# Strassen's rule for the output projection of the mixers in a two-layer encoder

## The chip, the cores and the metric

The kernel runs on one core of a Trainium2 chip. The metric is the device time of one execution in microseconds, the median of several runs. The engines of the core are named as in the profile: PE does matmuls (PEld is its weight load), DVE and ACT are the vector and the scalar engine, POOL and SP here mostly issue DMAs.

## The reference

The program is the trunk of an encoder: 16 learned tokens are put before 512 input tokens (528 rows of 1024 features), two layers follow, and a norm at the end.

```python
for l in range(DEPTH):                       # DEPTH = 2, D_MODEL = 1024, D_FF = 2816
    h = h + 0.5 * swiglu(rmsnorm(h, g[l, 0]), w_gate[l, 0], w_up[l, 0], w_down[l, 0])
    h = h + mixer(rmsnorm(h, g[l, 1]), ...)
    h = h + 0.5 * swiglu(rmsnorm(h, g[l, 2]), w_gate[l, 1], w_up[l, 1], w_down[l, 1])
return rmsnorm(h, final_norm)[:, N_META:]

def mixer(z, ...):                           # a, b: 528 x 512 each
    a, b = gla_branch(...), attention_branch(...)
    y = sigmoid(g_a + b_merge[0]) * (a @ w_pa) + sigmoid(g_b + b_merge[1]) * (b @ w_pb)
    return y @ w_out                         # y: 528 x 1024, w_out: 1024 x 1024
```

All is float32. This case is about the last line, `y @ w_out`.

## The kernel before

Activations lie transposed: a chunk of h is 128 features by all tokens (528; in the mixer of the last layer and after it only the 512 that the output needs), and there are 8 chunks. A float32 product is done as three: operand and weights are split into a high part that PE takes as it is and a low part with the rest, and high x high, high x low and low x high are added in PSUM. The helper `split` does it for operands (ACT casts at L476, DVE subtracts at L477), `Weights.make` for a slab of weights of 128 x 1024 (ACT `whi` at L310, DVE `wlo` at L311). Slabs come by DMAs that SP issues (L287, or `block` for the FFN), a few slabs ahead of their use. The order of use is a list made ahead, `weight_plan`, which `W.next` and `W.op` walk.

The FFNs already use Strassen's rule in the Winograd form. The operand of the FFN's first products is made by `Norm.pair` out of two finished chunks of h: seven slices (`xc`, high and low), each a quarter or a sum of quarters. Seven products numbered "1" to "7" replace eight, each with a weight block that is a quarter (11, 12, 22 for "1", "2", "4") or a sum of quarters. These sums are made outside PE: partly on DVE, partly by DMAs from POOL that add into their target (`add`, L224), with negations on ACT (L219). The FFN's last products (`fast_down`, L745) do the same with three groups of merged gate and up values, in two halves of the output columns each (`dq` 0 and 1); a group is 4, 4 or 3 pairs long, and each product adds its PSUM result into h (L753).

The end of the mixer is plain. For m in 0 to 7 the two gates of a chunk are made, `pa` and `pb` are products of four slabs each (L1255, L1256), the gates are multiplied with them on DVE (L1259), added (L1261) and split (L476, L477). Then, for each of the 8 chunks of output, eight slabs of `w_out` are multiplied with the eight chunks of y (L1267; the matmuls are at L488), the result is added into h (L587) and `done(m)` is called: a square of the chunk on ACT (L522) and a sum of squares on DVE (L526), and after every second chunk `pair`, which makes the slices for the next FFN (L532 to L551). The next FFN begins with the matmuls at L621.

Each engine serves its instructions in order; the order is that in which the program is written, changed by a scheduler within priorities.

Of the kernel before, what the change touches and what calls it, by code (L numbers as in the profile page):

```python
# [10 lines left out]
F32 = mybir.dt.float32  # L11
# [30 lines left out]
GROUPS = (4, 4, 3)  # L42
ALL_FAST = [(0, 0), (1, 0)]
# [16 lines left out]
def ffn_steps(f):  # L60
# [3 lines left out]
    for g, n in enumerate(GROUPS):  # L64
# [7 lines left out]
        for i in range(n):  # L72
# [5 lines left out]
            if not more and g < fast:  # L78
# [7 lines left out]
                turns = [("S", g, *t, 3) for t in zip(AB, "16273465734")]  # L86
# [16 lines left out]
def weight_plan():  # L103
# [20 lines left out]
    for l in range(DEPTH):  # L124
# [37 lines left out]
NOP = NPAIR + QUADS * len(GROUPS)  # L162
# [20 lines left out]
def wide(i):  # L183
    return SLAB if i < NPAIR else 2 * P * GROUPS[(i - NPAIR) // QUADS]


class Weights:
# [93 lines left out]
    def fetch(self, upto):  # L281

        while self.fetched < min(upto, len(self.loads)):
            load = self.loads[self.fetched]
            if isinstance(load, int):
                w = self.raw.tile([P, SLAB], F32, tag="raw", name=f"raw{load}")
                self.nc.sync.dma_start(w, self.wts[load])  # L287
                self.raws[self.fetched] = w
            elif load[2] in DIRECT:
# [62 lines left out]
def build(tc, ctx, xt, wts, win, par, w2, const, umask, out):  # L352
# [240 lines left out]

    pending, closing = [load_constants], [None]

    def ffn(l, f, norm, done, following):
# [67 lines left out]
        def hidden(st, p, m):  # L664
# [11 lines left out]
            if p < sum(GROUPS[:fast]):  # L676
                if p // 4 not in raw:
                    raw[p // 4] = [quarter("g") for _ in range(4)]
                for q in range(2):
# [7 lines left out]
        def quarter(tag, dtype=F32):  # L687
            return slots[tag].tile([P, 2 * T], dtype, tag=tag, name=nm(tag))[:, : 4 * w].rearrange(
                "p (k c) -> p k c", k=4)

        def operand(g, c, ks=None):

            ks = ks or slice(0, GROUPS[g])
            src = raw[g][{"1": 0, "2": 2, "5": 0, "6": 0, "7": 1, "3": 3, "4": 2}[c]]
            if (g, c) not in sets:
                tag = "c" if c in "56" else "g"
                sets[g, c] = [quarter(tag, F32R) for _ in range(2)]
            hi, lo = [t[:, ks] for t in sets[g, c]]
            if c == "3":
                S.activation(hi, src[:, ks], AF.Copy, scale=-1.0)  # L700
                V.scalar_tensor_tensor(lo, src[:, ks], -1.0, hi.bitcast(F32), ALU.mult, ALU.subtract)
            else:
                cast = S.copy(hi, src[:, ks])
                if g == len(GROUPS) - 1:
                    prev_act[0] = cast.ins
                V.tensor_tensor(lo, src[:, ks], hi.bitcast(F32), ALU.subtract)  # L706

        def difference(g, into, a, b, ks=None):
            r, ks = raw[g], ks or slice(0, GROUPS[g])
            V.tensor_tensor(r[into][:, ks], r[a][:, ks], r[b][:, ks], ALU.subtract)  # L710

        def operands_of(g, ks, order):
            for c in order:
                if c == "5":
                    difference(g, 0, 1, 0, ks)
                operand(g, c, ks)

        def operands_behind(g, dq, c):
            if (dq, c) == (1, "1"):
                difference(g, 1, 1, 3)  # L720
                operand(g, "7")
            elif (dq, c) == (1, "2"):
                operand(g, "3")
                difference(g, 2, 2, 0)
                operand(g, "4")

        def fast_down(g, dq, c, part):
            last = sum(GROUPS[: g + 1]) - 1
            kinds = ("ss", "s2") if last % 2 == 0 else ("s2", "ss")
            st = made.setdefault(("S", g, dq), {})  # L730
            where = {"2": "Y", "5": "Z", "3": "Z"}.get(c, "X")
            begin = c in "125"
            if part != 2:
                if begin:
                    st[where] = pair(kinds[{"Y": 0, "Z": 1, "X": dq}[where]] == "s2")
                st["w"] = st.get("w", {})
                st["w"][c] = W.op((l, f), NPAIR + QUADS * g + dq, c, ahead=AHEAD_MADE - 1)
            acc = st[where][:, :, :w]
            hi, lo = st["w"][c]
            xs = sets[g, c]  # L740
            n = GROUPS[g]
            for k in {1: range(n - 1), 2: range(n - 1, n), 3: range(n)}[part]:
                for j in range(2):
                    for i, (a, b) in enumerate(((hi, 0), (hi, 1), (lo, 0))):
                        closing[0] = TE.matmul(acc[:, j], a[:, j, k], xs[b][:, k], start=bool(begin and k == 0 and i == 0),  # L745
                                               stop=k == n - 1 and i == 2, skip_group_check=not begin).ins
            if part == 1:
                return
            st["w"].pop(c)
            for m, q in {"1": [(0, 0)], "2": [(0, 0)], "5": [(1, 1)], "6": [(0, 1)], "3": [(0, 1)], "7": [(1, 1)],  # L750
                         "4": [(1, 0)]}[c]:
                to = hall[:, 4 * dq + 2 * m : 4 * dq + 2 * m + 2, q * w : (q + 1) * w]
                V.tensor_tensor(to, to, acc, ALU.add)  # L753
            if g == len(GROUPS) - 1:
                if c in "34":
                    ready.extend([4 * dq + 2 * (c == "4"), 4 * dq + 2 * (c == "4") + 1])
                for _ in range(len(ready) if (dq, c) == CLOSING[-1] else min(len(ready), PACE)):
                    m = ready.pop(0)
                    lower_h(m, rs)
                    done(m)  # L760
            if dq == 1:
                sets.pop((g, c))
            with tc.high_priority() if c == "1" else nullcontext():
                operands_behind(g, dq, c)
# [24 lines left out]
        for i, step in enumerate(steps):  # L789
# [16 lines left out]
            elif step[0] == "O":  # L806
                g, last = step[1:]
                n_k = GROUPS[g]
                ks = slice(n_k - 1, n_k) if last else slice(0, n_k - 1)
                operands_of(g, ks, "152")  # L810
                difference(g, 0, 3, 0, ks)
                if last:
                    for ks in (slice(0, 2), slice(2, n_k)):
                        operand(g, "6", ks)
# [365 lines left out]
    def mixer(l, norm, done, following):  # L1180
# [67 lines left out]
        y = []  # L1248
        for m in range(KC):
            ga, gb = gates[2 * m : 2 * m + 2]  # L1250
# [183 lines left out]
```

## Time and profile before

| | |
|---|---|
| median of 3 runs | 2187.26 us (2186.92 to 2187.61) |
| span of the profiled execution | 2185.6 us |
| PE, DVE, ACT, POOL busy | 2149.1, 1802.6, 1245.9, 119.0 us |
| end of the mixer of layer 0: merge, projection | 676.5 to 718.9, 718.9 to 765.6 us |
| projection of layer 1 | 1791.8 to 1836.2 us |

Times are from the start of the span. "idle before" and the brackets name what ended a wait of the engine. A matmul's printed length is longer than the distance from one matmul to the next, since they are pipelined; distances are the safer number. The granted TensorE clock (PEclk) is 1.00 in the stages spoken of here.

### The profile page before, as it was taken

The numbers are of one execution on the slowest core, as the hardware profiler recorded it, in microseconds if no ns is written. First come the engines' busy times: TensorE is split into PE (matmuls) and PEld (weight loads), VectorE is DVE, ScalarE is ACT, GpSimd is POOL, SyncE is SP. The second block draws the span as 40 slices with busy tenths as digits, with TensorE's granted clock in tenths as the row PEclk, the third lists the DMA queues.
The fourth block names the chain that finished last, engine by engine and source line by source line (L and its number), as shares of the span: only waits on it lengthen the run. The fifth ranks groups of instructions, "written<-read, shape, count | busy, mean of one in ns | idle before, by whom it ended". The sixth has DMA issues, their size and how long they took to land.

```text
span 2185.6 us, 40161 instructions
## 1 busy us (share of the span) xinstructions
PE 2149.1 (98%) x16434; PEld 2056.1 (94%) x16434; DVE 1802.6 (82%) x2751; ACT 1245.9 (57%) x1844; POOL 119.0 (5%) x140
## 2 busy tenths in 40 slices
PE   7999999999999999999999999999999999999998
PEld 7999999989999999999999999988788888999997
DVE  8887979776976689888789979797779767997986
ACT  8545556444784556454575455574557836554544
POOL 1100000000000000010010000000000001000100
PEclk9999999999999999999999999999999999999999
DMA  9866755212113467676567667553121146775751
GB/s 286 218 195 182 202 154 139 82 51 76 49 40 123 130 177 180 202 185 183 167 162 187 199 181 204 153 140 97 49 78 49 49 135 152 199 204 178 196 162 68
DMA packets 91223, 320.32 MB, mean 147 GB/s; under 512 B 10144, under 2 KB 12576, under 8 KB 91040
## 3 DMA queue, kind: packets, MB, share of 16 engines
q1 hardware_dynamic: 70048, 246.58, 33.9%
q0 software_dynamic: 19584, 69.21, 17.6%
q8 instruction: 129, 2.11, 0.4%
q10 hardware_dynamic: 1408, 1.97, 0.3%
q14 instruction: 54, 0.44, 0.1%
HBM read 294.65 MB, written 2.10 MB: 136 GB/s over the span
## 4 chain that ended last, share of the span: by engine, by line
PE 83%; DVE 9%; ACT 4%; DMA 2%; issue 2%; SPq 0%; DVEq 0%; ACTq 0%
PE ss L621 36%; PE mm L488 15%; PE ss L745 14%; PE ss L488 7%; DVE wlo L311 3%; PE sm L488 2%; DMA w<-win 2%; PE sm L1125 1%; PE ss L1100 1%; ACT whi L310 1%; PE ss L494 1%; DVE h L753 1%; PE sm L1141 1%; PE ss L1101 1%; PE sm L1142 1%
## 5 line engine op out<-in xcount | busy, mean ns | idle before, releaser
L621 PE MATMUL ss<-xc,whi 128*128 128x264 f32 (+1 forms) x4928 | 903.1, 285 | 11.3 <-ACT whi L310 7.4
L621 PEld LDWEIGHTS ss<-xc,whi 128*128 128x128 f32 x4928 | 764.5, 189 | 14.9 <-ACT whi L310 8.0
L621 PE MATMUL ss<-xc,wlo 128*128 128x264 f32 (+1 forms) x2464 | 700.6, 285 | 4.0 <-DVE wlo L311 4.0
L311 DVE TENSOR_TENSOR wlo<-w,whi 128x1024 fp32r<-128x1024 f32 (+2 forms) x355 | 423.7, 1200 | 66.7 <-ACT whi L310 66.3
L621 PEld LDWEIGHTS ss<-xc,wlo 128*128 128x128 f32 x2464 | 465.0, 189 | 5.9 <-DVE wlo L311 5.9
L310 ACT CAST whi<-w 128x1024 fp32r<-128x1024 f32 (+2 forms) x355 | 362.1, 1036 | 169.3 <-PE ss L621 80.1
L488 PE MATMUL mm<-x,whi 128*128 128x264 f32 (+1 forms) x1712 | 385.5, 315 | 0.0
L488 PEld LDWEIGHTS mm<-x,whi 128*128 128x128 f32 x1712 | 278.1, 188 | 16.3 <-issue 1.0
L745 PE MATMUL ss<-g,whi 128*128 128x264 f32 (+1 forms) x1520 | 284.3, 285 | 3.6 <-DVE h L753 1.7
L488 PE MATMUL mm<-x,wlo 128*128 128x264 f32 (+1 forms) x856 | 266.3, 316 | 0.0
L745 PEld LDWEIGHTS ss<-g,whi 128*128 128x128 f32 x1520 | 236.2, 188 | 7.5 <-DVE g L706 3.6
L745 PE MATMUL ss<-g,wlo 128*128 128x264 f32 (+1 forms) x760 | 215.2, 283 | 0.0
L625 ACT COPY c<-ss 128x528 f32<-128x528 f32 (+1 forms) x132 | 78.4, 594 | 239.0 <-PE ss L621 238.7
L310 ACT CAST whi<-raw 128x1024 fp32r<-128x1024 f32 x114 | 119.3, 1048 | 130.7 <-PE mm L488 94.2
L311 DVE TENSOR_TENSOR wlo<-raw,whi 128x1024 fp32r<-128x1024 f32 x114 | 139.0, 1220 | 57.2 <-ACT whi L310 53.2
L488 PEld LDWEIGHTS mm<-x,wlo 128*128 128x128 f32 x856 | 159.6, 188 | 8.5 <-issue 0.5
L745 PEld LDWEIGHTS ss<-g,wlo 128*128 128x128 f32 x760 | 143.0, 188 | 0.0
L224 POOL DMA_DIRECT2D w<-win x64 | 56.1, 876 | 1453.2 <-DVE t L1261 342.0
L745 PE MATMUL ss<-c,whi 128*128 128x264 f32 (+1 forms) x608 | 115.5, 285 | 0.3
L311 DVE TENSOR_TENSOR wlo<-s,whi 128x1024 fp32r<-128x1024 f32 (+1 forms) x94 | 112.2, 1195 | 1.6 <-ACT whi L310 1.4
L467 ACT ACTIVATE c<-c 128x528 f32<-128x528 f32 (+1 forms) x88 | 56.5, 642 | 98.5 <-DVE c L671 98.4
L488 PE MATMUL ss<-g,whi 128*128 128x264 f32 (+2 forms) x516 | 103.6, 310 | 0.0
(270 smaller groups left out, 3379.1 us busy)
## 6 DMA issues: line engine op xcount, KB each, us to landing
w<-win SPq DMA_DIRECT2D x333, 512.0 KB, 4.4
raw<-wts SPq DMA_DIRECT2D x114, 512.0 KB, 3.3
w<-win POOLq DMA_DIRECT2D x60, 512.0 KB, 7.5
s<-win POOLq DMA_DIRECT2D x26, 512.0 KB, 7.5
w<-s POOLq DMA_DIRECT2D x26, 512.0 KB, 6.1
w<-win SPq DMA_DIRECT2D x20, 384.0 KB, 3.6
s<-w POOLq DMA_DIRECT2D x8, 512.0 KB, 7.4
h<-xt SPq DMA_DIRECT2D x3, 528.0 KB, 6.0
```

The source lines that it names most:

```text
L224: self.nc.gpsimd.dma_start(t, src, accum_op=ALU.add)
L310: nc.scalar.copy(hi[:, cs], w[:, cs])
L311: nc.vector.tensor_tensor(lo[:, cs], w[:, cs], hi[:, cs].bitcast(F32), ALU.subtract)
L467: prev_act[0] = S.activation(*args, **kw).ins
L488: TE.matmul(acc.half[i][:width], lhs, rhs[:, acc.spans[i]], start=first, stop=last)
L494: TE.matmul(a, weights, x[:, hs], start=True, stop=True)
L621: TE.matmul(acc[:, j], a[:, j, k], b[:, at], start=bool(begin and k == 0 and i == 0), stop=k == len(x) - 1 and i == 2, skip_group_check=no ...
L625: W.behind = S.copy(part(st, q), acc).ins
L745: closing[0] = TE.matmul(acc[:, j], a[:, j, k], xs[b][:, k], start=bool(begin and k == 0 and i == 0), stop=k == n - 1 and i == 2, skip_gro ...
L753: V.tensor_tensor(to, to, acc, ALU.add)
L1100: TE.matmul(s[:n, i, :HF], lhs, kh[:, hs], start=True, stop=False)
L1101: TE.matmul(s[:n, i, :HF], lhs, kl[:, hs], start=False, stop=True)
```

## The change

The output projection becomes one more group of the scheme that `fast_down` uses. The code of that scheme moves, unchanged in what it does, from the FFN into a class `Sets`, which the FFN and the mixer share. In the mixer

- the merged values of a chunk are not split any more, but written as two token halves into raw quarters (`raw[0]` to `raw[3]`, L1284): chunks with even m into quarters 0 and 1, with odd m into 2 and 3;
- `Sets.operand` and `Sets.difference` make the operands of the seven products out of them: "1", "5", "2" in `begin` (three of the four places of a quarter before m = 6, the last place after the merge loop, and then "6"), "7", "3", "4" behind products of the second column half;
- the projection is 7 products times two column halves, 24 matmuls each, in the order of `MERGED` after (0,"1"), (0,"5") and (0,"2"); 18 matmuls of (0,"1") stand ahead of the last pair of `pa` and `pb`. A product's result goes into two chunks of h at once for half of the tokens (L673, 14 adds of 128 x 2 x 264). `done` follows after products "3" and "4", one chunk per product;
- `w_out` is laid out as quarters. For each column half SP loads five blocks, and four DMAs from POOL add one block into another. One sum is made when the block of "6" has been split: ACT negates the block 12 (L281), and POOL adds block of "6" into it; the result is the weight of "3". The block buffers are opened ahead of the merge loop.

```diff
-        y = []
+        close_pools(pools)
+        opened()
+        own = open_pools("left", c=4)
+        raw = [quarter("c") for _ in range(4)]
+        out = Sets((l, 1), OUT, raw, ("ss", "s2"), {"4": "c"})
+        w = n_out // 2
         for m in range(KC):
+            if m == KC - 2:
+                out.begin(False)
+            if m == KC - 1:
+                out.product(0, "1", 1)
...
-            t = slot("t")
-            V.tensor_tensor(t, ga, gb, ALU.add)
-            y.append(split(t, "g"))
-        close_pools(pools)
+            for q in range(2):
+                cs = slice(q * w, (q + 1) * w)
+                V.tensor_tensor(raw[2 * (m % 2) + q][:, m // 2], ga[:, cs], gb[:, cs], ALU.add)
+        close_pools(banks)
         close_pools(norm.pools)
+        own.update(open_pools("left", psum=("s2",), s2=2))
         following()
-        for m in range(KC):
-            add_to_h(m, product("w_out", Acc(KINDS[m % 4]), y, KC))
-            done(m)
-        close_pools(banks)
+        for c in "52":
+            out.product(0, c, 1)
+        out.begin(True)
+        for c in "152":
+            out.product(0, c, 2)
+        ready = []
+        for dq, c in MERGED:
+            out.product(dq, c, 3)
+            if ready:
+                done(ready.pop(0))
+            if c in "34":
+                ready += [4 * dq + 2 * (c == "4"), 4 * dq + 2 * (c == "4") + 1]
+        for m in ready:
+            done(m)
+        close_pools(own)
```

and, in the class that the FFN shares (its bodies are those that stood in the FFN before):

```diff
+    class Sets:
+        def operand(self, c, ks=None):
...
+                cast = S.copy(hi, src[:, ks])
...
+                V.tensor_tensor(lo, src[:, ks], hi.bitcast(F32), ALU.subtract)
+        def difference(self, into, a, b, ks=None):
+            r, ks = self.raw, ks or slice(0, self.n)
+            V.tensor_tensor(r[into][:, ks], r[a][:, ks], r[b][:, ks], ALU.subtract)
+        def behind(self, dq, c):
+            if (dq, c) == (1, "1"):
+                self.difference(1, 1, 3)
+                self.operand("7")
+            elif (dq, c) == (1, "2"):
+                self.operand("3")
+                self.difference(2, 2, 0)
+                self.operand("4")
+        def product(self, dq, c, part):
...
+                to = hall[:, 4 * dq + 2 * m : 4 * dq + 2 * m + 2, q * w : (q + 1) * w]
+                V.tensor_tensor(to, to, acc, ALU.add)
```

and where the order of the products and the weights is set:

```diff
+MERGED = tuple(zip((1, 0, 1, 0, 0, 0, 1, 1, 1, 1, 1), "16273465734"))
...
+            if m == KC - 1:
+                plan.append(("op", (l, 1), NPAIR + QUADS * OUT, "1"))
             mat("w_pa", (l,), m * P, 0, 4)
             mat("w_pb", (l,), m * P, 0, 4)
-        for m in range(KC):
-            mat("w_out", (l,), m * P, 0, KC)
+        for dq, c in ((0, "5"), (0, "2")) + MERGED:
+            plan.append(("op", (l, 1), NPAIR + QUADS * OUT + dq, c))
```

How this moves instructions, in layer 0. The names: `h` is the residual stream, `xc` the slices of a pair for the next FFN, `wlo` and `whi` the parts of a weight block, `w_01_18`, `s_01_18` a block or a sum of blocks of the second column half of `w_out` (17 is the first), `w_01_0`, `s_01_0` those of the next FFN's first pair of columns, `c` and `g` in the last columns quarters and operands, `t` scratch.

DVE, the end of the projection. Before, the rows between the slices of the third pair (xc_9137) and those of the fourth (xc_9280):

```order
L540 TENSOR_TENSOR xc_9137<-t_9145,xc_9136 128x528
L587 TENSOR_TENSOR h<-h,ss_9154 128x528
L526 TENSOR_TENSOR t_8780<-t_8780,t_9211 128x528
L311 TENSOR_TENSOR wlo_9217<-w_01_1_8870,whi_9216 128x1024
L587 TENSOR_TENSOR h<-h,sm_9214 128x264
L587 TENSOR_TENSOR h<-h,sm_9215 128x264
L526 TENSOR_TENSOR t_8780<-t_8780,t_9272 128x528
L547 TENSOR_TENSOR t_9287<-t_9275 128x264
L548 TENSOR_TENSOR t_9287<-t_9276,t_9287 128x264
L540 TENSOR_TENSOR xc_9280<-t_9275,xc_9279 128x264
L540 TENSOR_TENSOR xc_9280<-t_9276,xc_9279 128x264
```

In the change, between the third (here xc_9270) and the fourth (here xc_9298):

```order
L551 SCALAR_TENSOR_TENSOR xc_9270<-t_9266,xc_9269 128x264
L554 TENSOR_TENSOR t_9277<-t_9266,t_9277 128x264
L556 TENSOR_TENSOR t_9278<-t_9265,t_9266 128x264
L557 TENSOR_TENSOR t_9278<-t_9266,t_9277 128x264
L532 TENSOR_TENSOR t_9051<-t_9051,t_9287 128x528
L546 TENSOR_TENSOR xc_9270<-t_9277,xc_9269 128x528
L546 TENSOR_TENSOR xc_9270<-t_9278,xc_9269 128x528
L532 TENSOR_TENSOR t_9051<-t_9051,t_9290 128x528
L553 TENSOR_TENSOR t_9305<-t_9293 128x264
L317 TENSOR_TENSOR wlo_9325<-w_01_1_9015,whi_9324 128x1024
L546 TENSOR_TENSOR xc_9298<-t_9293,xc_9297 128x264
L546 TENSOR_TENSOR xc_9298<-t_9294,xc_9297 128x264
```

Before, the last products of the projection and the chunks they finish take turns; now four sums of squares and two pairs of slices stand one behind another after the last add into h (L673, six rows further up in that listing).

ACT, where the sums of the weights are negated. Before, in the middle of the projection:

```order
L522 ACTIVATE t_8930<-h 128x528
L310 CAST whi_8935<-raw_8596 128x1024
L219 ACTIVATE s_01_0_8722<-w_01_0_8720 128x1024
L522 ACTIVATE t_8991<-h 128x528
L532 ACTIVATE t_8994<-h,par 128x528
L532 ACTIVATE t_8995<-h,par 128x528
L539 CAST xc_8998<-t_8994 128x264
L539 CAST xc_8998<-t_8995 128x264
L544 ACTIVATE xc_8998<-t_8995 128x264
```

In the change:

```order
L528 ACTIVATE t_9051<-h 128x528
L528 ACTIVATE t_9084<-h 128x528
L223 ACTIVATE s_01_0_8943<-w_01_0_8941 128x1024
L281 ACTIVATE s_01_18_8981<-w_01_18_8541 128x1024
L538 ACTIVATE t_9087<-h,par 128x528
L538 ACTIVATE t_9088<-h,par 128x528
L545 CAST xc_9091<-t_9087 128x264
L545 CAST xc_9091<-t_9088 128x264
L550 ACTIVATE xc_9091<-t_9088 128x264
L545 CAST xc_9091<-t_9099 128x528
L528 ACTIVATE t_9139<-h 128x528
L316 CAST whi_9110<-s_01_18_8981 128x1024
```

`s_01_18_8981` is the weight of (1,"3"): it is negated behind the squares of the first two chunks of h (t_9051, t_9084), and cast (whi_9110) behind the first pair's slices.

PE, where the FFN first needs the fourth pair. In the change:

```order
L706 MATMUL ss_9355<-xc_9269,wlo_9226 128x264
L706 MATMUL ss_9355<-xc_9269,whi_9225 128x264
L706 MATMUL ss_9355<-xc_9270,whi_9225 128x264
L706 MATMUL ss_9355<-xc_9269,wlo_9226 128x264
L706 MATMUL ss_9388<-xc_9091,whi_9324 128x264
L706 MATMUL ss_9388<-xc_9092,whi_9324 128x264
L706 MATMUL ss_9323<-xc_9297,whi_9196 128x264
L706 MATMUL ss_9355<-xc_9297,whi_9225 128x264
L706 MATMUL ss_9388<-xc_9091,wlo_9325 128x264
```

Row by row, 38 matmuls of the FFN stand ahead of the first with xc_9297, the fourth pair; before, 27 stand ahead of it. Over the whole program PE has 16279 matmuls for 16183, DVE 2797 instructions for 2743, ACT 1814 for 1788, POOL 152 DMAs for 136, SP 486 for 482.

More of the change, by code (lines that the diff above doesn't have):

```diff
@@ L42 @@
 GROUPS = (4, 4, 3)
+OUT = len(GROUPS)
+SETS = GROUPS + (KC // 2,)
 ALL_FAST = [(0, 0), (1, 0)]
@@ L85, in ffn_steps @@
                     continue
-                turns = [("S", g, *t, 3) for t in zip(AB, "16273465734")]
+                turns = [("S", g, *t, 3) for t in MERGED]
                 steps += turns[:6]
@@ L161 @@
 NPAIR = FF // P // 2
-NOP = NPAIR + QUADS * len(GROUPS)
+NOP = NPAIR + QUADS * len(SETS)
 PLAN = weight_plan()
@@ L183, in wide @@
 def wide(i):
-    return SLAB if i < NPAIR else 2 * P * GROUPS[(i - NPAIR) // QUADS]
+    return SLAB if i < NPAIR else 2 * P * SETS[(i - NPAIR) // QUADS]
 class Weights:
@@ L288, in fetch @@
                 self.raws[self.fetched] = w
+            elif self.short is None:
+                return
             elif load[2] in DIRECT:
@@ L678, in hidden @@
                     raw[p // 4] = [quarter("g") for _ in range(4)]
+                    last = LAST[p // 4] % 2 == 0
+                    sets[p // 4] = Sets((l, f), p // 4, raw[p // 4], ("ss", "s2") if last else ("s2", "ss"), {"5": "c", "6": "c"})
                 for q in range(2):
@@ L685, in hidden @@
             hid[2 * p + m] = split(u, "g")
[L687 to L725, printed above, removed]
@@ L727, in fast_down @@
-        def fast_down(g, dq, c, part):
[L728 to L747, printed above, removed]
-                return
[L749 to L759, printed above, removed]
-                    done(m)
[L761 to L764, printed above, removed]
@@ L766, in down @@
+        def fast_down(g, dq, c, part):
+            sets[g].product(dq, c, part)
+            if part == 1 or g < len(GROUPS) - 1:
+                return
+            if c in "34":
+                ready.extend([4 * dq + 2 * (c == "4"), 4 * dq + 2 * (c == "4") + 1])
+            for _ in range(len(ready) if (dq, c) == CLOSING[-1] else min(len(ready), PACE)):
+                m = ready.pop(0)
+                lower_h(m, rs)
+                done(m)
         def down(g, m, first, last):
@@ L807, in ffn @@
                 g, last = step[1:]
[L808 to L814, printed above, removed]
+                sets[g].begin(last)
             else:
@@ L1178, in block_pools, with mixer @@
         return pools
-    def mixer(l, norm, done, following):
+    def mixer(l, norm, done, opened, following):
         x, n_out = norm.x, T if l < DEPTH - 1 else SEQ
@@ L1259, in mixer @@
                     V.tensor_tensor(cut(gate), cut(gate), pv, ALU.mult)
[L1260 to L1263 removed]
+            for q in range(2):
+                cs = slice(q * w, (q + 1) * w)
+                V.tensor_tensor(raw[2 * (m % 2) + q][:, m // 2], ga[:, cs], gb[:, cs], ALU.add)
+        close_pools(banks)
         close_pools(norm.pools)
+        own.update(open_pools("left", psum=("s2",), s2=2))
         following()
[L1266 to L1267 removed]
+        for c in "52":
+            out.product(0, c, 1)
+        out.begin(True)
+        for c in "152":
+            out.product(0, c, 2)
[4 more added lines that the diff above has]
+                done(ready.pop(0))
+            if c in "34":
+                ready += [4 * dq + 2 * (c == "4"), 4 * dq + 2 * (c == "4") + 1]
+        for m in ready:
             done(m)
[L1269 removed]
+        close_pools(own)
     fin = Norm(G_FIN)
@@ L1352, in build @@
         close_pools(bp.pop())
-        mixer(l, b, c.chunk_of_pair, lambda: (operand_pools(c, "xc"), bp.append(block_pools())))
+        W.long = W.short = None
+        mixer(l, b, c.chunk_of_pair, lambda: bp.append(block_pools()), lambda: operand_pools(c, "xc"))
         if l < DEPTH - 1:
@@ L1404 @@
         row += 2 * P * n
+    wo = a["w_out"].reshape(DEPTH, KC // 2, 2, P, QUADS, 2, 2, P).transpose(0, 4, 5, 2, 3, 6, 1, 7).reshape(DEPTH, 1, -1, P, SLAB)
+    blocks.append(np.pad(wo, [(0, 0), (1, 0)] + [(0, 0)] * 3))
     win = np.ascontiguousarray(np.concatenate(blocks, axis=2)).reshape(-1, P, SLAB)
```

52 lines of the change are left out of this document (51 added, 1 removed).

## The prediction

> **What bounds the kernel now.** I read the page's first part, then a table of busy time by stage, since the change touches two places of some 45 us, then PE's waits there.
>
> ```profile
> PE 2149.1 (98%) x16434; PEld 2056.1 (94%) x16434; DVE 1802.6 (82%) x2751; ACT 1245.9 (57%) x1844; POOL 119.0 (5%) x140
> ```
>
> PE is busy for 98% of the span, so matmuls that go are worth their full time, as long as nothing makes PE wait. DVE at 82% isn't far behind. The stages, with columns as in the first line:
>
> ```profile
> core 0: us, PE busy (x) PEld busy (x) DVE busy (x) ACT busy (x) POOL busy (x), PEclk, DMA share, GB/s
> 676.50:718.90 42.40, 42.40 (x347) 42.40 (x347) 29.13 (x45) 14.00 (x18) 0.89 (x1) 1.00 0.44 137
> 718.90:765.60 46.70, 46.70 (x388) 46.70 (x386) 31.73 (x56) 26.19 (x40) 4.36 (x5) 1.00 0.55 141
> 1791.80:1836.20 44.40, 44.40 (x193) 35.87 (x191) 30.51 (x52) 25.75 (x40) 4.37 (x5) 1.00 0.55 140
> 330.00:380.00 50.00, 48.68 (x390) 47.69 (x389) 49.36 (x74) 34.08 (x50) 3.22 (x4) 1.00 0.50 132
> ```
>
> The first is the merge of layer 0, the next two are the output projections of layers 0 and 1: PE never stops in them, and DVE idles for a third of the time. The last is the end of the first FFN, whose last products go by Strassen's rule already: there DVE is full and PE loses 1.3 us. At the end of the two projections PE waits once each:
>
> ```profile
> PE ss L621 <- DVE wlo L311: 0.5, 1, 0.5
> ...
> PE ss L621 <- DVE wlo L311: 0.8, 1, 0.8
> ```
>
> **What the matmuls that go are worth.** Layer 0: 384 matmuls, 264 wide, in 46.70 us make 0.1216 us each. Strassen does seven products of 3 x 4 x 2 matmuls for each of two column halves, 336, also 264 wide. 48 x 0.1216 = **5.8 us**. Layer 1: 192 matmuls, 512 wide, in 44.40 us (0.231 each) become 336 that are 256 wide. For that width I take the second layer's next FFN:
>
> ```profile
> 1859.99 0.40 PE L621 MATMUL ss<-xc,whi 128*128 128x256 f32 x2
> ...
> 1861.05 0.40 PE L621 MATMUL ss<-xc,whi 128*128 128x256 f32 x2
> ```
>
> Between these lie nine matmuls (three groups of whi, whi, wlo) in 1.06 us, 0.118 each; 336 x 0.118 = 39.6, so 44.4 - 39.6 = **4.8 us**. Together 10.6 us.
>
> [...] The trace has 231 and 118 ns, a ratio of 0.51, and I go by it.
>
> **What DVE gets.** Halving the number of PE's products costs DVE: operands must be added, split into high and low part, and seven results per half added into h (14 adds of 528 instead of 8 of 528 or pairs of 264); there are 14 weight blocks instead of 8, each with a low half on DVE. And these come after the last gate product: three of the four merged quarters are complete only then. To see whether DVE keeps up, I count its instructions in the new order, in layer 0, from the last gate product to the first slice of the fourth pair of the next FFN's operand (xc_9298), which PE needs after all 318 products that remain of the projection (18 of the 336 stand ahead of the last gate product) and 38 of the FFN. They are 78: 14 low halves of 1024, 29 of 528 (14 adds to h, 7 sums of squares, 8 of the operands), 30 of 264, 5 of 1056. What each takes on a full queue shows where they stand back to back:
>
> ```profile
> 793.99 1.22 DVE L271 TENSOR_TENSOR w<-w,w 128x1024 f32<-128x1024 f32 x1
> 795.13 0.42 DVE L681 TENSOR_TENSOR g<-c,ss 128x264 f32<-128x264 f32 x1
> 795.47 0.42 DVE L681 TENSOR_TENSOR g<-c 128x264 f32<-128x264 f32 x1
> 795.81 0.70 DVE L654 TENSOR_TENSOR c<-c,ss 128x528 f32<-128x528 f32 x1
> 796.43 1.22 DVE L320 TENSOR_TENSOR w<-w,w 128x1024 f32<-128x1024 f32 x1
> ...
> L706 DVE TENSOR_TENSOR g<-g,g 128x1056 fp32r<-128x1056 f32 x12 | 15.0, 1247 | 0.0
> ```
>
> From start to start: 1.14 for 1024, 0.34 for 264, 0.62 for 528; each is some 0.085 shorter than its printed length, so 1056 takes 1.247 - 0.085 = 1.16. 14 x 1.14 + 29 x 0.62 + 30 x 0.34 + 5 x 1.16 = 16.0 + 18.0 + 10.2 + 5.8 = **49.9 us**. In layer 1 each row is 1 to 3% shorter (512 for 528); I take 49.0. PE's work up to there is (318 + 38) x 0.1216 = **43.3 us**, in layer 1 356 x 0.118 = **42.0**. DVE's queue is served in order, so PE must wait for it: at least 6.6 and 7.0 us. In the kernel before, the same stretch has 62 DVE instructions (8 of 1024, 19 of 528, 35 of 264), 32.8 us at these lengths, against 46.7 us of projection and 27 FFN matmuls; that is why it showed only 0.5 and 0.8.
>
> If the lengths as printed held instead (1.22, 0.70, 0.42, 1.25), the queue would be 56.2 us, 6.3 more in each layer; the rows above show the overlap, so I take the lower end.
>
> **What else delays that queue.** Three hand-overs where DVE has just caught up with PE or ACT (the start, the operand of "7", one product's end) at about 0.3 each, an estimate between gaps such as these two; 0.9 in all, between 0 and 3 x 0.77:
>
> ```profile
> 792.85 1.23 DVE L311 TENSOR_TENSOR wlo<-w,whi 128x1024 fp32r<-128x1024 f32 x1 [0.18 <-ACT whi L310]
> ...
> 767.87 0.71 DVE L526 TENSOR_TENSOR t<-t,t 128x528 f32<-128x528 f32 x1 [0.77 <-ACT t L522]
> ```
>
> Then the last weight sum. The block of (1,"3") of the second half is a chain: ACT negates a block (s_01_18_8981), POOL adds another into it by DMA, ACT casts it, DVE takes the low half, as 44th of the 78. In ACT's order this negation stands behind two squares of finished chunks of h (L528 of the change), and these wait for the adds that DVE makes at 22.0 us into its queue.
>
> ```profile
> L522 ACT ACTIVATE t<-h 128x528 f32<-128x528 f32 x40 | 24.1, 636 | 12.3 <-DVE h L587 12.2
> L219 ACT ACTIVATE s<-w 128x1024 f32<-128x1024 f32 x34 | 35.7, 1056 | 6.9 <-DMA w<-win 3.6 <-DVE wlo L311 3.0
> L310 ACT CAST whi<-w 128x1024 fp32r<-128x1024 f32 x333 | 344.7, 1051 | 157.2 <-PE ss L621 75.9 <-PE ss L745 47.5 <-DVE wlo L311 9.3
> ...
> 1436.95 0.84 ACT L277 ACTIVATE s<-w 128x768 f32<-128x768 f32 x1 [0.40 <-DVE wlo L311]
> ...
> 1438.20 0.88 POOL L224 DMA_DIRECT2D s<-w  x1 [5.79 <-ACT s L277]
> ...
> s<-w POOLq DMA_DIRECT2D x8, 512.0 KB, 7.4
> ...
> DMA to landing us min/median/max: 3.8/7.5/11.7
> ```
>
> 22.0 plus 0.6 of hand-over, two squares (1.3), the FFN's negation ahead of it and its own (2.1): 26.0; POOL issues 0.41 after a negation ends (1437.79 to 1438.20): 26.4; landing 7.4 later: 33.8; cast: 34.9. DVE has reached the low half at 30.4 + 0.9 = 31.3. It stands there for **3.5 us**, and behind it all of pairs 1 to 3 of the next FFN. For the landing the ends are 3.8 and 11.7: 0 to 7.8 us lost.
>
> [...]
>
> Behind the fourth pair DVE and ACT are still late: walking the rows on at these durations, PE waits once more for each of two weight blocks' low halves, 1.5 and 0.9 us; I take **2.4**, between 0 and 2.4.
>
> **What I cost at nothing.** In the merge, a split and a 528-wide add per m become two adds of 264: less for DVE, and PE is the bound there (42.40 of 42.40 busy). Four more loads on SP and 16 more DMAs on POOL: the DMA share is 0.44 to 0.55 in these stages, and the loads of the first blocks lie ahead of the merge, as the block buffers are opened there now. If that cover is gone, a late block costs a landing, 7.4 us at most. ACT gets 26 instructions more in all, at 57% busy.
>
> **The sum** (layer 0, layer 1): queue 49.9, 49.0; hand-overs 0.9 each; late sum 3.5 each: 54.3, 53.4. Less PE's work 43.3, 42.0: PE stands for 11.0, 11.4. Tail 2.4 each. Less the waits of before, 0.5 and 0.8, less the matmuls, 5.8 and 4.8: +7.1, +8.2. Together +15.3 us on a span of 2185.6, that is 2200.9; the median of the runs lies 1.7 over that span: **2203 us**.
>
> **The rivals.**
> 1. DVE is the bound, but the sum lands in time (landing at 3.8, or ACT comes to the negation sooner). For it: 3.8 is in the row; against it the median. 15.3 - 2 x 3.5 = +8.3: **2196**.
> 2. DVE keeps pace, as in the FFN's end at 330 to 380, which has the same scheme, a DVE busy for 49.36 of 50 us, and a PE that loses 1.3. Then 10.6 saved less 2 x 1.3: -8.0, **2179**. It decides where the queue takes less than PE's work plus what is saved and the wait of before: 43.3 + 5.8 + 0.5 = 49.6 in layer 0, 47.6 in layer 1. Against it: 49.9 and 49.0 lie above that without one hand-over. And the stage at 330 to 380 shows a DVE that just fits, 49.36 in 50, not one with 49.9 for 43.3.
> 3. Only the queue counts, with no hand-over, no late sum and no tail: +0.3 and +1.4, **2189**, no difference that shows.
> 4. The sums land at 11.7: 2 x 4.3 more: **2212**.
>
> **How the numbers follow.** 0.55 for 2203, 0.22 for rival 1, 0.10 for rival 2, 0.08 for rival 3, 0.05 for rival 4. About 0.2%, 4.4 us, is what a measurement of this kernel can tell from no change. Faster: rival 2 and a little beyond, 0.11; the same: rival 3, 0.09; slower: 0.80. The range goes from rival 3 to rival 4, 2189 to 2212, and leaves out rival 2.
>
> **What would show it.** Right: in each layer PE stands about 11 us in the first 40 matmuls of the second FFN, waiting for xc or wlo of DVE; DVE is full from the last gate product to there but for one wait of 3 to 4 us on ACT's cast of the late sum; the projection's own matmuls keep 0.122 and 0.118. Wrong: PE busy across that place (then DVE's rows are shorter or were done earlier), or stalls inside the projection, ahead of the products (then weights or operands are late, not the queue as a whole).

## The result, and the profile after

The change makes the kernel slower: 2202.5 us median (2201.6 to 2202.8, 5 runs) for 2187.3 before, ratio 1.0066, 95% interval 1.0054 to 1.0078. 2203 us were forecast. The span of the profiled execution is 2201.0 for 2185.6 us, 15.4 us more (forecast: 15.3).

Where it went shows from the same places of the program in both traces. The rows are matmuls that both kernels have, start and length first: one in the first mixer ahead of the changed place, the first norms after the changed places of layer 0 and ahead of that of layer 1, and the last norm. Before:

```profile
555.62 0.38 PE L1066 MATMUL ss<-t,const 128*128 128x16 f32 x2
...
1132.76 1.13 PE L494 MATMUL ss<-t,const 128*128 128x264 f32 x4 [1.05 <-DVE t L526]
1597.12 1.05 PE L494 MATMUL ss<-t,const 128*128 128x264 f32 x4
2167.27 0.70 PE L1295 MATMUL ss<-t,const 128*128 128x256 f32 x2
```

After:

```profile
557.08 0.37 PE L1079 MATMUL ss<-t,const 128*128 128x16 f32 x2
...
1140.89 1.13 PE L500 MATMUL ss<-t,const 128*128 128x264 f32 x4 [1.08 <-DVE t L532]
1605.37 0.83 PE L500 MATMUL ss<-t,const 128*128 128x264 f32 x3
2183.14 0.70 PE L1329 MATMUL ss<-t,const 128*128 128x256 f32 x2
```

The differences are 1.5, 8.1, 8.3 and 15.9 us. So layer 0 costs 6.7 us (forecast 7.1), layer 1 7.6 (forecast 8.2), and 1.5 us are gone before the change is reached. Those 1.5 us aren't shown to be the change's: of the kernels below, the two that run the code of before up to there have the first row 2.3 us (the stalls, 557.92) and 1.0 us (the DVE load) later than before, and the early sum, which runs the code of the change up to there, has it at 555.56, as before.

Busy time over the page and the stages of the change, after (columns as before: us, PE, PEld, DVE, ACT, POOL, granted clock, DMA share, GB/s):

```profile
PE 2150.3 (98%) x16530; PEld 2063.0 (94%) x16530; DVE 1838.3 (84%) x2805; ACT 1269.9 (58%) x1870; POOL 133.0 (6%) x156
...
722.00:754.00 32.00, 32.00 (x265) 32.00 (x264) 30.86 (x43) 20.87 (x26) 3.16 (x4) 1.00 0.50 132
758.60:764.80 6.20, 5.75 (x24) 5.44 (x25) 6.20 (x12) 6.04 (x10) 0.00 (x0) 0.50 0.88 259
772.00:775.00 3.00, 3.00 (x14) 3.00 (x15) 3.00 (x8) 2.73 (x6) 0.87 (x1) 0.50 1.03 251
1802.00:1833.00 31.00, 31.00 (x264) 30.96 (x263) 30.14 (x42) 20.56 (x26) 2.77 (x4) 1.00 0.47 124
```

The matmuls run at the pace forecast: 32.00 us / 265 = 0.121, and 31.00 / 264 = 0.117 at 256 wide. DVE is full, 30.9 of 32 us where it was 31.7 of 46.7. New are the two rows with a clock of 0.50. What PE waits for between the last gate product and the FFN's first results (total us, times, longest), layer 0 and the longest of layer 1:

```profile
PE ss L665 <- ACT whi L316: 3.5, 1, 3.5
PE ss L706 <- ACT xc L545: 1.2, 1, 1.2
PE ss L706 <- DVE xc L546: 0.9, 1, 0.9
PE ss L706 <- ACT c L710: 0.7, 1, 0.7
PE ss L706 <- DVE wlo L317: 0.5, 1, 0.5
PE ss L665 <- DVE wlo L317: 0.5, 1, 0.5
PE ss L706 <- ACT whi L316: 0.4, 1, 0.4
...
PE ss L665 <- ACT whi L316: 4.1, 1, 4.1
```

L665 is a product of the projection, (1,"3"): PE itself stands there, before it comes to the FFN. The 0.7 us for c is a wait that the kernel before has too (0.69 at 788.67). Where PE stands at the start of the FFN (its first matmul starts at 767.73):

```profile
770.63 0.39 PE L706 MATMUL ss<-xc,whi 128*128 128x264 f32 x1 [1.23 <-ACT xc L545]
771.91 0.59 PE L706 MATMUL ss<-xc,whi 128*128 128x264 f32 x1 [0.89 <-DVE xc L546]
...
777.58 0.39 PE L706 MATMUL ss<-xc,wlo 128*128 128x264 f32 x1 [0.49 <-DVE wlo L317]
```

The first two are the FFN's 13th and 14th matmul, which take the third pair. And the path of the late sum, on ACT, POOL and DVE, with the fourth pair at the end:

```profile
722.07 0.77 DVE L1281 TENSOR_TENSOR g<-g,sm 128x264 f32<-128x264 f32 x2 [1.60 <-PE sm L494]
...
746.55 1.04 ACT L281 ACTIVATE s<-w 128x1024 f32<-128x1024 f32 x1
...
748.00 0.87 POOL L228 DMA_DIRECT2D s<-w  x1
...
757.49 1.04 ACT L316 CAST whi<-s 128x1024 fp32r<-128x1024 f32 x1 [6.63 <-DMA s<-w]
...
752.80 0.70 DVE L532 TENSOR_TENSOR t<-t,t 128x528 f32<-128x528 f32 x1
758.57 1.22 DVE L317 TENSOR_TENSOR wlo<-s,whi 128x1024 fp32r<-128x1024 f32 x1 [5.07 <-ACT whi L316]
...
777.44 0.77 DVE L546 TENSOR_TENSOR xc<-t,xc 128x264 fp32r<-128x264 f32 x2
```

DVE begins the last gate product at 722.07. It reaches the sum's low half 31.3 us later (752.80 + 0.62 = 753.4; forecast 31.3), stands 5.07 us (forecast 3.5), and has the two first slices of the fourth pair at 778.2, 56.1 us after its start (forecast 54.3). Without the wait for the sum that is 51.0 us: 50.5 of work (forecast 49.9) and two hand-overs of 0.5 together (forecast 0.9).

### The profile page after: what moved, and what is told of

Same layout as the page of the kernel before. It is cut to its first block, busy times and chain, and to the rows that moved or that the text cites. A ratio compares the mean times of both kernels' runs of the same rounds, so it can differ in the third digit from the quotient of the medians.

```text
span 2201.0 us, 40528 instructions
## 1 busy us (share of the span) xinstructions
PE 2150.3 (98%) x16530; PEld 2063.0 (94%) x16530; DVE 1838.3 (84%) x2805; ACT 1269.9 (58%) x1870; POOL 133.0 (6%) x156
## 4 chain that ended last, share of the span: by engine, by line
PE 79%; DVE 13%; ACT 4%; issue 2%; DMA 2%; SPq 0%; DVEq 0%; ACTq 0%
PE ss L706 36%; PE ss L665 15%; PE mm L494 14%; PE ss L494 5%; DVE wlo L317 4%; PE sm L494 2%; DVE h L673 1%; PE sm L1138 1%; DMA s<-w 1%; DMA w<-win 1%; PE ss L1113 1%; DVE g L625 1%; PE ss L500 1%; ACT whi L316 1%; PE sm L1154 1%
## 5 line engine op out<-in xcount | busy, mean ns | idle before, releaser
L706 PE MATMUL ss<-xc,whi 128*128 128x264 f32 (+1 forms) x4928 | 908.5, 286 | 18.1 <-ACT whi L316 7.8
L706 PEld LDWEIGHTS ss<-xc,whi 128*128 128x128 f32 x4928 | 767.7, 189 | 23.3 <-ACT whi L316 8.3
L706 PE MATMUL ss<-xc,wlo 128*128 128x264 f32 (+1 forms) x2464 | 702.2, 285 | 3.4 <-DVE wlo L317 3.3
L317 DVE TENSOR_TENSOR wlo<-w,whi 128x1024 fp32r<-128x1024 f32 (+2 forms) x375 | 448.8, 1204 | 64.6 <-ACT whi L316 64.0
L316 ACT CAST whi<-w 128x1024 fp32r<-128x1024 f32 (+2 forms) x375 | 382.5, 1037 | 185.8 <-PE ss L706 83.3
L706 PEld LDWEIGHTS ss<-xc,wlo 128*128 128x128 f32 x2464 | 466.7, 190 | 5.3 <-DVE wlo L317 5.2
L665 PE MATMUL ss<-g,whi 128*128 128x264 f32 (+1 forms) x1904 | 357.8, 287 | 11.4 <-ACT whi L316 7.6
L665 PEld LDWEIGHTS ss<-g,whi 128*128 128x128 f32 x1904 | 298.7, 190 | 15.8 <-ACT whi L316 9.6
L665 PE MATMUL ss<-g,wlo 128*128 128x264 f32 (+1 forms) x952 | 271.2, 285 | 0.9 <-DVE wlo L317 0.9
L665 PEld LDWEIGHTS ss<-g,wlo 128*128 128x128 f32 x952 | 181.0, 190 | 1.5 <-DVE wlo L317 1.5
L316 ACT CAST whi<-raw 128x1024 fp32r<-128x1024 f32 x98 | 102.5, 1048 | 124.3 <-PE mm L494 88.0
L317 DVE TENSOR_TENSOR wlo<-raw,whi 128x1024 fp32r<-128x1024 f32 x98 | 119.6, 1222 | 38.0 <-ACT whi L316 33.9
L665 PE MATMUL ss<-c,whi 128*128 128x264 f32 (+1 forms) x672 | 127.3, 285 | 0.4
L673 DVE TENSOR_TENSOR h<-h,ss 128x528 f32<-128x528 f32 (+1 forms) x168 | 115.4, 696 | 6.7 <-PE ss L665 6.0
L316 ACT CAST whi<-s 128x1024 fp32r<-128x1024 f32 (+1 forms) x102 | 105.6, 1035 | 24.3 <-DMA s<-w 13.2
```

The source lines that it names most:

```text
L316: nc.scalar.copy(hi[:, cs], w[:, cs])
L317: nc.vector.tensor_tensor(lo[:, cs], w[:, cs], hi[:, cs].bitcast(F32), ALU.subtract)
L706: TE.matmul(acc[:, j], a[:, j, k], b[:, at], start=bool(begin and k == 0 and i == 0), stop=k == len(x) - 1 and i == 2, skip_group_check=no ...
```

## The experiments

All are compared with the kernel before on the same chip; the intervals are those of the ratio to it.

**The sum early.** Theory A is that of the prediction, theory S says that the late sum is the whole cause.

```diff
             if not isinstance(load, int) and load[2] in "126":
                 self.sums(*load, w)
+            if not isinstance(load, int) and load[1:] == (NPAIR + QUADS * OUT, "7"):
+                self.last_sum(load[0], load[1] + 1, self.summed[load[0], load[1] + 1, "6"])
```

(`last_sum` is the negation and the DMA of before, made once.)

> The change, with one edit: the weight sum of (1,"3") is begun behind the block of (0,"7"), some 9 us before its place in the change, so that it lies ready when DVE comes to it. Theory A (DVE's queue is the bound, the late sum adds the 5.1 us for which DVE stands in each layer): about 5 us less in each layer, 2192 us (2189 to 2196), PE no longer stands for 3.7 us inside the projection and the clock stays at 1.00 there, but still waits at the start of the next FFN. Theory S (the late sum alone is the cause, DVE would keep pace without it): 2178. Theory C (the sum is hidden by the queue, whatever it does): 2202.

Measured: 2191.6 us (2189.4 to 2194.0), ratio 1.0020, 1.0011 to 1.0030. As theory A has it. PE waits nowhere inside the projection any more; at the start of the FFN it still does:

```profile
PE ss L716 <- ACT xc L555: 2.3, 1, 2.3
PE ss L716 <- DVE h L683: 1.0, 1, 1.0
...
772.61 0.42 DVE L561 SCALAR_TENSOR_TENSOR xc<-t,xc 128x264 fp32r<-128x264 f32 x1
```

That row stands right behind the fourth pair's first two slices: 772.6 less DVE's start at 721.9 is 50.7 us, DVE idle for 0.3 of them. So the late sum cost 5.4 us a layer, 10.9 of the 15.2 us in all, and what is left is DVE's full queue, or something of the same length. ACT could be that as well: it is full where PE's longest wait falls (2.3 us for a high slice, which ACT makes, at 765.73):

```profile
761.00:770.00 9.00, 5.70 (x34) 5.32 (x35) 8.67 (x17) 9.00 (x17) 2.63 (x3) 0.88 0.89 210
```

**Without the low halves.** The early sum again; DVE makes no low halves of the projection's weight blocks, and the low x high part of the product is left out.

```diff
-                nc.vector.tensor_tensor(lo[:, cs], w[:, cs], hi[:, cs].bitcast(F32), ALU.subtract)
+                if isinstance(load, int) or load[1] < NPAIR + QUADS * OUT:
+                    nc.vector.tensor_tensor(lo[:, cs], w[:, cs], hi[:, cs].bitcast(F32), ALU.subtract)
+                else:
+                    lo = hi
```

> As the one before, and the low halves of the output projection's 14 weight blocks per layer aren't made on DVE: PE multiplies with the high half a second time in their place (same matmuls, the low x high part of the sum is left out). This takes 16 us off DVE's queue of 49.9 us. Theory A (the queue as a whole is the bound): 34 us of DVE against 43.3 of PE, so PE doesn't wait, all of the 10.6 us saved comes out: 2178 (2176 to 2181). Theory B (the end of the chain is the bound: the last two pairs of the next FFN are made only after the last product of the projection, some 8 to 9 us on DVE and ACT, while PE has 38 matmuls, 4.6 us): about 4 us of waiting stay in each layer, 2186 (2184 to 2190).

Measured: 2186.9 us (2184.9 to 2188.6), ratio 0.9998, 0.9988 to 1.0007. Theory B's 2186, not theory A's 2178. Busy time up to the end of the projection, and from there to where the fourth pair is used:

```profile
721.00:760.30 39.30, 38.88 (x320) 38.67 (x318) 29.56 (x49) 31.71 (x43) 4.89 (x6) 1.00 0.71 179
760.30:772.00 11.70, 9.92 (x72) 9.07 (x72) 11.49 (x24) 9.80 (x19) 1.21 (x2) 1.00 0.91 211
...
761.48 0.69 DVE L686 TENSOR_TENSOR h<-h,ss 128x528 f32<-128x528 f32 x1
...
769.16 0.77 DVE L559 TENSOR_TENSOR xc<-t,xc 128x264 fp32r<-128x264 f32 x2
```

DVE now has 10 us to spare ahead of the last product, and is full behind it: from the last add into h (761.48) it takes 8.4 us to the fourth pair's slices (769.9). They come 48.9 us after DVE's start, only 1.8 us sooner than with the full queue, against 43.3 us of matmuls. So there are two bounds of nearly one length: DVE's work as a sum (49.9), and the end behind the last product (38.7 us of matmuls, then two pairs, three squares and two low halves of the FFN's first blocks), where ACT is busy for 9.8 of the 11.7 us too. 16 us off the first bring 4.7 us in both layers together.

**The same DVE load, put on the kernel before.**

```diff
+            if isinstance(load, int) and load in self.loaded:      # the slabs of w_out
+                for _ in range(3):
+                    nc.vector.tensor_tensor(w, w, w, ALU.max)
             self.got[s] = (hi, lo)
```

> The kernel before, with three needless DVE operations of 1024 behind each of the eight weight slabs of the output projection. From the last gate product to the first slice of the fourth pair DVE then has 49.6 us of work by the same lengths, as much as in the change (49.9), but PE has the 50.0 us of matmuls of before, and the products come in the order of before. Theory A (a wait comes only where DVE's sum is over PE's): 49.6 and 0.9 of hand-overs against 50.0, 0.5 to 1 us lost in each layer for 0.5 and 0.8 now: 2188 (2187 to 2190). If a DVE that is full costs PE also where the sums are equal, since each add, low half and slice comes late by what stands ahead of it: 3 to 6 us in each layer, 2193 to 2199.

Measured: 2211.7 us (2210.6 to 2212.4), ratio 1.0109, 1.0092 to 1.0126: far from both. The trace shows what the expectation overlooked:

```profile
721.05 0.41 PE L492 MATMUL sm<-x,wlo 128*128 128x264 f32 x2
...
729.04 0.77 DVE L1263 TENSOR_TENSOR g<-g,sm 128x264 f32<-128x264 f32 x2
...
779.70 0.77 DVE L544 TENSOR_TENSOR xc<-t,xc 128x264 fp32r<-128x264 f32 x2
```

Nine of the extra operations are served ahead of the last gate product, as blocks are split ahead of their use, and DVE comes to it 7.8 us after PE has ended (721.2). From there the queue takes 51.4 us to the fourth pair, which is 49.6 of work and 1.5 idle, near enough. So the sum along the queue holds, but it begins when DVE does, not when PE does. In the change DVE waited for PE at that place (the row at 722.07, 1.60), so there it was right to start both at once. The run shows the length of the queue; the 12 us a layer that it costs aren't broken down here, and a lower clock is among them (0.83 from 770 to 790 us, 1.00 from 720 to 770).

**The squares elsewhere.** Two kernels make the squares for the norm inside the FFN:

```diff
-        mixer(l, b, c.chunk_of_pair, ...)
+        mixer(l, b, c.pair_of, ...)
```

> The early sum, and the squares for the next norm are made inside the FFN, where the kernel does so already between two FFNs, not behind each finished chunk: 7 sums of 528, 4.3 us, leave DVE's queue ahead of the fourth pair. All is computed. Theory A: queue 45.6 and 0.9 of hand-overs against 43.3 us of PE, 3.2 us lost in each layer: about 2184 (2181 to 2187), a little faster than before. Theory B: the end behind the last product gets 2.5 us shorter, about the same. Theory S: 2178.

Measured, with the early sum: 2192.6 us (2190.0 to 2195.5), ratio 1.0026, 1.0016 to 1.0035; no better than the early sum alone. The 4.3 us off the queue don't come out: the longest wait at the start of the FFN in layer 1 is a single one of 4.8 us for ACT's part of a slice.

> The change with the squares inside the FFN alone, the sum where the change has it. ACT comes to the negation some 1.2 to 2 us sooner, and DVE's queue is 4.3 us shorter, of which 3.1 behind the late sum. Theory A: 2202.5 - 2 x (2 + 3.1) = 2192 (2189 to 2196), with PE still standing at (1,"3") for 2 to 4 us. Theory S: 2202.5 - 2 x 2 = 2198.

Measured, with the sum as in the change: 2200.2 us (2198.0 to 2202.0), ratio 1.0061, 1.0044 to 1.0077. Nearer to what was expected of theory S (2198) than of A (2192), but S is out by the first run; PE still stands 3.3 us at (1,"3"), and behind it as before.

**A shorter end.** In the projection (1,"3") goes ahead of (1,"7"), and the pairs of the last chunks are made before the last squares:

```diff
-        for dq, c in MERGED:
+        for dq, c in LATER:                  # ... (1,6) (1,5) (1,3) (1,7) (1,4)
             out.product(dq, c, 3)
-            if ready:
+            for _ in range(min(len(ready), 2 if (dq, c) == (1, "7") else 1)):
                 done(ready.pop(0))
...
         for m in ready:
-            done(m)
+            done.__self__.pair_of(m)
+        for m in ready:
+            done.__self__.square(m)
```

> The early sum, and the end of the chain loosened: in the projection (1,"3") comes ahead of (1,"7"), the two chunks that it finishes are handed over behind (1,"7"), so that the third pair of the next FFN is made during (1,"4") and only the fourth is left behind the last product, and the last two squares come behind the fourth pair. DVE's work up to the fourth pair stays nearly what it was: 48.7 us and 0.9 of hand-overs against PE's 43.3. Theory A (the queue as a whole): 6.3 us are still lost in each layer, and the time is that of the early sum alone less some 2: 2189 (2187 to 2192). Theory B (the end behind the last product): from the last add into h to the fourth pair's slices only some 3 us are left for 8 to 9, less than PE's 4.6 us of matmuls there: 2180 (2178 to 2183).

Measured: 2197.0 us (2195.4 to 2197.4), ratio 1.0043, 1.0026 to 1.0060, above all that was expected. The waits of PE name it:

```profile
PE ss L676 <- DVE h L684: 3.3, 1, 3.3
PE ss L717 <- ACT whi L325: 2.4, 1, 2.4
```

L676 is (1,"4"): it adds to the same PSUM tile as (1,"7"), and may do so only when DVE has added that tile to h. In the change (1,"3") stands between the two and hides the add; here PE waits for it, behind a full queue. Three more kernels stand on the same order and carry the same flaw, so they don't test theory B as meant.

> The one before, and all squares for the norm inside the FFN: 45.6 and 0.9 against 43.3 us. Theory A: 3.2 us lost in each layer, 2185 (2182 to 2188). Theory B: as the one before, 2180. If squares inside the FFN cost there what they save here, as the run with late squares and the early sum makes likely, 2189.

Measured, squares inside the FFN as well: 2194.0 us (2191.5 to 2196.0), ratio 1.0028, 1.0017 to 1.0039.

> Both bounds taken away at once: early sum, looser end, squares inside the FFN, and no low halves of the projection's weight blocks on DVE (PE uses the high half twice; the low x high part of the sum is left out). If A and B are all there is: 2178 (2175 to 2181), that is the 10.6 us of matmuls less 1 to 2 of hand-overs. If something else eats the gain (the FFN behind, the clock, the weights' arrival), it stays at 2183 or above.

Measured: 2191.4 us (2188.2 to 2195.2), ratio 1.0016, 1.0007 to 1.0026; even without low halves PE waits 2.4 us in layer 0 at (1,"4").

With the change's own order of products, and the last three squares behind the pairs alone:

> The early sum, with the change's order of products, and the squares of the last three chunks behind the slices of the fourth pair, 1.9 us of DVE less between the last product and these slices. Theory B (the end behind the last product): the wait at the start of the FFN gets 1.9 us shorter in each layer, 2188 (2186 to 2190) for 2191.6 with the early sum alone. If that wait isn't on the path, or the squares are missed later by the norm: 2191 or more.

Measured: 2193.4 us (2190.6 to 2194.8), ratio 1.0025, 1.0015 to 1.0035, not better than the early sum alone.

> The one before without the low halves of the projection's weight blocks on DVE (PE uses the high half twice; the low x high part of the sum is left out), to be set beside the early sum without low halves, 2186.9. Theory B: 1.9 us less in each layer, 2183 (2181 to 2186). If what is left there are hand-overs of half a us to a us between PE, DVE and ACT, as that run's trace suggests, not one wait at the end: 2187 (2185 to 2189).

Measured: 2191.6 us (2189.2 to 2193.0), ratio 1.0019, 1.0010 to 1.0029, worse than without this edit (2186.9). In its trace PE waits 2.1 us for ACT's cast of the FFN's next block, which stands behind those squares on ACT: the work put behind the pairs is ahead of the blocks that PE needs next. So the end isn't one chain that can be cut at DVE: from 760.5 to 772.5, behind the last product, DVE is busy for 11.5 and ACT for 10.0 of 12 us, and what is put off makes something else late.

**Work moved to POOL.** This stands on the kernel with the shorter end and the squares inside the FFN (2194.0 us), which its expectation calls the one before.

```diff
+            (nc.gpsimd if self.g == OUT and (ks.start, ks.stop) == (0, self.n) else V).tensor_tensor(r[into][:, ks], r[a][:, ks], r[b][:, ks], ALU.subtract)
...
+                here = not isinstance(load, int) and (load[1] - NPAIR - QUADS * OUT, load[2]) in ((0, '7'), (0, '3'))
+                (nc.gpsimd if here else nc.vector).tensor_tensor(lo[:, cs], ...)
```

> The one before, and 4.6 us of DVE's queue moved to POOL, which is idle there: the two differences for the operands of "7" and "4" (1056 wide) and the low halves of two weight blocks, (0,"7") and (0,"3"). Queue 41 and 0.9 against 43.3 us. Theory A: the queue isn't the bound any more, 2180 (2177 to 2184), faster than before. How long POOL takes for such a subtraction no run has shown; if it takes three times DVE's time or slows DVE beside it, operands and blocks come late and it is 2187 or more.

Measured: 2201.4 us (2199.8 to 2201.9), ratio 1.0061, 1.0046 to 1.0076; 7 us more than without POOL. POOL and DVE in its trace:

```profile
724.42 5.23 POOL L641 TENSOR_TENSOR c<-c,c 128x1056 f32<-128x1056 f32 x2
729.30 2.66 POOL L327 TENSOR_TENSOR wlo<-s,whi 128x1024 fp32r<-128x1024 f32 x1
738.68 2.73 POOL L327 TENSOR_TENSOR wlo<-s,whi 128x1024 fp32r<-128x1024 f32 x1
...
724.33 8.82 DVE L637 TENSOR_TENSOR g<-c,g 128x528 fp32r<-128x528 f32 x2
739.15 3.38 DVE L637 TENSOR_TENSOR c<-c,c 128x1056 fp32r<-128x1056 f32 x1
```

POOL takes 2.7 us where DVE takes 1.14, and while it works DVE's subtractions are held up: two of 528 took 8.8 us for 1.3, one of 1056 took 3.4 for 1.25.

**The price of a stall.** In the kernel before, PE is held up by extra copies on ACT:

```diff
+            if m in stalls:                              # ({1: 0, 5: 3}, {1: 1, 5: 6})[l]
+                t = slot("t")
+                S.activation(t, h(m - 1), AF.Copy, scale=0.0)
+                for _ in range(stalls[m]):
+                    S.activation(t, t, AF.Copy)
+                S.activation(y[0][0], y[0][0].bitcast(F32), AF.Identity, bias=t[:, 0:1], scale=1.0)
```

> The kernel before, with PE held up on purpose at four products of the output projection: its operand's high half is rewritten (same values) by ACT behind 1, 4, 2 and 7 short copies that begin when the product before has been added to h; estimates of the stalls are 2.3 and 5 us in layer 0 and 2.9 and 6.5 us in layer 1. If a stall costs its length alone: 16 to 18 us more, 2204. If the clock falls to half for some microseconds behind a stall: 2 to 4 us more for each that is long enough, 2207 to 2213, with matmuls at 0.22 and not 0.12 us apart behind it, and the four lengths show from which length on.

Measured: 2221.1 us (2219.6 to 2222.1), ratio 1.0155, 1.0140 to 1.0170. The stalls came out longer than estimated, so that the total says little; the stages do, four stalls and what follows three of them:

```profile
726.30:729.90 3.60, 0.32 (x3) 0.10 (x1) 1.63 (x2) 1.91 (x3) 0.00 (x0) 1.00 0.38 145
753.30:761.80 8.50, 0.20 (x2) 0.00 (x0) 3.59 (x6) 6.27 (x10) 1.78 (x3) 0.64 0.70 158
761.90:766.00 4.10, 4.10 (x19) 4.10 (x20) 0.00 (x0) 0.00 (x0) 1.02 (x2) 0.50 0.96 184
1812.70:1817.00 4.30, 0.28 (x3) 0.00 (x1) 1.65 (x2) 2.50 (x4) 0.00 (x0) 1.00 0.32 122
1817.00:1820.50 3.50, 3.50 (x9) 2.73 (x10) 0.00 (x0) 0.00 (x0) 0.00 (x0) 0.54 0.00 0
1840.70:1851.30 10.60, 0.27 (x2) 0.00 (x0) 3.79 (x6) 8.34 (x13) 2.62 (x3) 0.68 0.76 163
1851.40:1855.00 3.60, 3.60 (x9) 2.91 (x10) 0.00 (x0) 0.00 (x0) 0.87 (x1) 0.52 1.06 212
```

Behind the stall of 3.3 us (some 3.6 between matmuls) nothing follows (two matmuls in 0.24 us from 730.55 on), behind those of 8.5, 4.3 and 10.6 the clock is about half: 19 matmuls in 4.1 us, 0.216 each for 0.1216, 1.8 us more; 9 of 512 in 3.5 us, 0.39 for 0.231, 1.4 us more; and 9 in 3.6 us, 1.5 us more. So in this run the stalls of 4.3, 8.5 and 10.6 us cost 1.4 to 1.8 us each on top. In the change the price is higher: behind the waits of 3.5 and 4.1 us at (1,"3") come 24 matmuls in 5.75 us and 20 in 4.74 (758.60 to 764.80 and 1838.20 to 1843.40, both at 0.50), 2.8 and 2.4 us more, within the 2 to 4 of the estimate. These four stalls don't show from which length on the clock falls: in other places it fell behind shorter waits (last section).

## Why the prediction was right, and what was wrong in it

**What bounds the kernel, and what the matmuls are worth: right.** 0.121 and 0.117 us were measured for 0.1216 and 0.118.

**DVE's queue: right in size, incomplete as a bound.** Its work from the start to the fourth pair was 50.5 us for 49.9 (layer 1: 49.5 for 49.0), its hand-overs 0.5 for 0.9. Taking 16 us off that queue, though, moved the fourth pair by 1.8 us only. The prediction took the queue for the one thing that sets that moment; the end behind the last product alone would set it at 48.9. It had the rows of this end in its count of 78, but not when they can begin: four of the eight chunks are finished by the last two products, so two pairs, squares and blocks are made after PE has only 38 matmuls left. The time came out right because both bounds are within 2 us of one another, which the prediction didn't know. ACT was set at nothing, with 57% of the span; from 757.5 to 775.4 us it is busy for 17.39 of 17.90 us, and no run tells what PE would wait for there with a faster ACT alone.

**The late sum: right mechanism, mis-sized landing.** Negation, issue and DVE's arrival were within 0.5 us (25.5, 25.9 and 31.3 us for 26.0, 26.4 and 31.3). The DMA took 9.4 us to land (748.00, cast at 757.49) for the 7.4 of the median row, so DVE stood 5.1 us for 3.5. Another sum had been issued 0.95 us ahead of it; whether that is why isn't shown. Rival 1 (2196) was then 4 us too high: with the sum early it is 2191.6.

**Where PE stands: partly wrong.** All was forecast at the start of the FFN, and stalls inside the projection were named as a sign against it. There is one, 3.5 and 4.1 us, with 0.5 more for the low half of the same block: the block that DVE waits for is the one that PE needs next. The rest, 3.0 us of named waits in layer 0 that the kernel before doesn't have, comes at the FFN, and not at the place that the prediction counted to. The 39th matmul there takes the fourth pair's high part (xc_9297), which ACT makes, not DVE's xc_9298; PE waits for the third pair (1.2 and 0.9 us) and for the low half that DVE makes just ahead of the fourth (0.5), so that its time is lost ahead of the fourth pair's low part. In layer 1 it also waits 1.2 us for a high slice of ACT, at 1855.65.

**The clock: not foreseen.** Behind these waits (3.5 us in the projection, 1.2 and 0.9 us at the FFN) it is 0.50, in layer 0 for 6.2 and 3.0 us of matmuls (38 in them). That is some 4 us of PE's time which the prediction had as waiting. With the early sum the half-clocked stretch inside the projection is gone along with the wait (1.00 from 721.9 to 761.9 us). Part of the 4 us lies where PE would have waited anyway: with the early sum it waits 3.6 us up to the third pair (1.0, 2.3 and 0.3) where it waits 2.1 in the change. How large that part is, no run shows.

**The tail of 2.4 us: too long.** At the fourth pair's first matmuls PE waits 0.5 us for a low half, and behind them 0.4 us (the rows of L706 for wlo and whi).

**How much of the number is luck.** The wait for the late sum was 1.6 us a layer longer than forecast and the tail of layer 0 was 1.5 us shorter, and the two all but cancel. The layers together cost 14.3 us for 15.3; the 15.4 of the whole span has in it the 1.5 us ahead of the change, which nothing in the prediction gives.

**The rivals.** DVE keeping pace (2179) is out: no kernel came near it, even with 16 us less on DVE. The queue alone (2189) is out by the early sum.

**What stays open.** Which of DVE and ACT sets the end behind the last product, and what makes up the 1.5 us ahead of the change. Whether an order of products exists that frees the end without two products on one PSUM tile behind one another wasn't found. No kernel that computes all beat the one before; the best, with the early sum, is 0.2% slower.

## What to carry to other kernels

A fast matrix scheme trades PE's time for another engine's, so it pays only where that engine has room between the moment its inputs are there and the moment its results are needed (here some 10.6 us of matmuls were saved and the two layers got 14.3 us longer); count its instructions in the order of the queue, from where it starts, not as a share of the span. Then count the same stretch a second time from its end: what can begin only after the last product is a bound of its own, and taking load off the queue doesn't shorten it (16 us off moved the fourth pair by 1.8 us). Two products that add to one PSUM tile need other work between them if the tile is read out in between: with (1,"4") right behind (1,"7") PE waited 3.3 us.

## What the runs showed of the hardware that was not expected

Beside tensor subtractions on POOL those on DVE were held up: two of 528 took DVE 8.8 us instead of 1.3 while POOL was busy for 5.2 and 2.7 us, one of 1056 took 3.4 instead of 1.25 beside one of 2.7 on POOL. What holds them up isn't shown. The 4.6 us taken from DVE so cost it some 9.6 us in these two places (7.5 and 2.1).

Behind five waits of PE of 3.5 to 10.4 us the clock was about half (0.50 to 0.54), which cost 1.4 to 2.8 us more each; behind one of 3.3 us, in the run with the stalls, it was not. It was half behind shorter waits too: 0.50 from 772 to 775 us in the change, behind waits of 1.2 and 0.9 us; and in the kernel without low halves and with the last squares behind the pairs the longest wait was 2.1 us, with one of 0.4 behind it, and the clock fell to 0.50 soon after. What decides whether it falls isn't shown.

```profile
771.30:773.40 2.10, 0.11 (x1) 0.00 (x0) 2.00 (x4) 2.10 (x5) 0.00 (x0) 1.00 0.12 23
775.60:778.80 3.20, 3.20 (x17) 3.20 (x16) 3.10 (x3) 1.22 (x3) 0.00 (x0) 0.50 0.41 143
```
